# One decoder layer on one core: V and output gate streamed together, GLA output one head later, other starts and ends of stages

## The chip, the cores and the metric

One NeuronCore of a Trainium2 chip runs one program. The metric is the device time of an execution in microseconds (us); lower is better. The kernel before has a median of 1220.12 us over 3 runs (1219.98 to 1223.33).

## What is computed

One layer of a hybrid decoder on x of 512 tokens by 1024 channels, all in float32 (batch 1, depth 1):

```python
h = rms_norm(x, norm_g[0]); proj = h @ w_in            # 1024 x 10816, cut into columns
y_a = rglru_mixer(...)   # conv of width 4, gates by blocks of 128, linear recurrence, GeLU gate
y_b = nsa_mixer(...)     # compressed, selected and window attention, 16 heads of 64
y_c = gla_mixer(...)     # 4 heads, key width 128, value width 256, chunks of 32, silu output gate
merged = sum(gates[i] * (y @ w_branch[i]))             # sigmoid merge gates, three branches
x = x + rms_norm(merged @ w_out, norm_g[1])
h = rms_norm(x, norm_g[2]); gt, up = split(h @ w_ffn_in)
x = x + rms_norm((silu(gt) * up) @ w_ffn_out, norm_g[3])  # d_ff = 2816
```

## The kernel before

All tokens stay on the chip; the weights are streamed. A **piece** of weights is 512 KB: 128 partitions of 1024 float32. SyncE issues its load into a `wraw` buffer (L82), ScalarE (ACT) copies it to a rounded fp32r half `whi` (L91), and VectorE (DVE) subtracts to the rest `wlo` (L92). There are 3 buffers of each, so piece n takes the buffers of piece n - 3. A product with full precision is three fp32r products (`mm3`, L121): high x high, high x low, low x high. Products whose operands were not split (transposes, small attention products) are plain fp32, which TensorE (PE) runs as two passes, each with an instruction of its own in the trace.

The stages, in order of time:
- **Front** (L246 to L309, to 17 us). Four loads bring x in blocks of 128 tokens (`xt0` to `xt3`), then two pieces `ck_raw`, and, from `load_w1(0)` (L391 to L394, called at L676), two loads of 1 MB of `cmp_w1` into the tile `M`, all on SyncE's queue in this order. PE multiplies zeros into a spare bank `WARM` = 14 times (L257). Each block is squared and summed on ACT (`square`), scaled on DVE (`root`, L283) and transposed on PE (L293) as it comes; then ACT and DVE make `hh` and `hl`, the high and low halves of h transposed.
- **NSA** (to 321 us). `small_proj` (L361) computes the 16 low-rank GLA columns and the branch gates; it first copies and adds the low-rank rows (`lr`, L370 to L376), then turns the gates around (`srev`, L379), transposes and gates them (L380 to L382). The attention loop follows with a hand-written order.
- **LRU** (to 477 us). The attention's PSUM pools are closed and others opened (L746 to L751). From here to L1208 the order on PE, DVE, ACT and GpSimd is the order of the code. `take()` (L815) hands out the next piece and has the piece two further split; `stream_t` (L825) multiplies two pieces of weights (stationary, 128x128) by `hh`/`hl` (moving, 512 columns), 48 products, and calls a function of its caller after each piece. `lru_params` (L893), which loads `wr`, makes the small `wa` and two tables of parameters, stands ahead of the loop; `lru_root` and `lru_scan(3)` stand behind it (L1034).
- **GLA** (to 644 us), four heads, each: a q/k stream (`stream_t`), `gla_qk` on DVE (L1052), the transposes of the head before (`gla_turn`, L1140), V by `stream_tok` (L844) with the tokens stationary and 256 columns of weights moving (96 products), `gla_scores` (L1078), the output gate by a second `stream_tok` (96 products), `gla_out` (state products `kvps`, states `ST`, outputs, L1104) and `gla_gate` (L1133). A head's psum tiles rotate through the 4 buffers of `pg`.
- **Merge**, **w_out and norms** (to 870 us), **first FFN product** (to 1100 us).
- **Second FFN product** (L1496 to L1624): a scheme with 7 block products instead of 8. The PSUM pools are closed (L1500) and 8 banks `acc` opened (L1539). `weights()` (L1478) hands out element i of a stream of 40 pieces and has element i + 2 split. The last block product, `p7`, ends with pieces that are held for both token halves (`w3`, L1608); behind its last product come the addition, `gain` (square and sum on ACT, times the norm's gain on DVE, in place), `mean`, `root` and `store` of the last two blocks.

Of the kernel before, what the change touches and what calls it, by code (L numbers as in the profile page):

```python
# [10 lines left out]
F32 = mybir.dt.float32  # L11
# [25 lines left out]
WARM = 14  # L37
# [25 lines left out]
def hybrid_block_kernel(ctx, tc, x, rel_table, norm_g, w_in, conv_w, conv_b, lru_w_gates, lru_b_gates,  # L63
# [181 lines left out]
    x1_d = dram.tile([128, TB, D], F32, name="x1_d")  # L245
    with tc.tile_pool(name="pre", bufs=1) as pp:  # L246
# [25 lines left out]
        with tc.manual_schedule(engines={mybir.EngineType.PE, mybir.EngineType.DVE, mybir.EngineType.Activation}):  # L272
# [88 lines left out]
    def small_proj(pp, ws):  # L361
# [4 lines left out]
        for k in range(8):  # L366
            pe.matmul(sps, w2[:, k], hh[:, k], start=k == 0, stop=False)
            pe.matmul(sps, w2[:, k], hl[:, k], start=False, stop=k == 7)

# [7 lines left out]
        gps = pt.tile([128, TB, 64], F32, name="gtps", tag="pt")  # L377
        srev = pp.tile([128, TB, 128], F32, name="srev", tag="psb", bufs=NPSB)
        v_.tensor_copy(srev, sps.rearrange("p (b c) -> p b c", b=TB)[:, :, ::-1])  # L379
        for tb in range(TB):  # L380
            pe.matmul(gps[:, tb], srev[:, tb], ii, start=True, stop=True)
        a_.activation(gates, gps[:, :, 16:64], AF.Sigmoid)  # L382
# [4 lines left out]
    M = mo_pool.tile([128, 8, S], F32, name="M")  # L387
# [358 lines left out]
    psum_ctx.close()  # L746
    psum_ctx = ExitStack()
    pg = psum_ctx.enter_context(tc.tile_pool(name="pg2", bufs=4, space=PSUM))
    gpools = [(pg, "g"), (pg, "g")]
    pa = psum_ctx.enter_context(tc.tile_pool(name="pa2", bufs=2, space=PSUM))  # L750
    pt = psum_ctx.enter_context(tc.tile_pool(name="pt2", bufs=2, space=PSUM))  # L751
# [31 lines left out]


# [5 lines left out]
    for h in range(4):  # L790
        pieces += in_pieces([(GLA_Q + h * 128, 128), (GLA_K + h * 128, 128)])
        pieces += in_pieces([(GLA_V + h * 256, 256)]) + in_pieces([(GLA_OG + h * 256, 256)])
# [51 lines left out]
    def stream_tok(act, *after):  # L844

        ps = [p.tile([128, 2, 256], F32, name="gps", tag=t) for p, t in gpools]
        both = [ps[tb // 2][:, tb % 2] for tb in range(TB)]
        for kh in range(2):
            for _ in steps_tok(both, take(), kh, act):
                pass  # L850
            if kh < len(after) and after[kh]:
                after[kh]()
        return ps
# [38 lines left out]

    def lru_params():  # L893
        sy.dma_start(wr, gla_wa2[0])
# [120 lines left out]
    lru_params()  # L1015
    for cp in range(4):
# [12 lines left out]
        gate_products(cp)  # L1029
        pm = stream_t(Y[:2], chain(lambda: lru_tanh(cp), *([z_products] if cp == 2 else [])),  # L1030
# [3 lines left out]
    lru_root()  # L1034
    lru_scan(3)
# [16 lines left out]
    def gla_qk(psq, psk, eb, KT, KE):  # L1052
# [3 lines left out]
        QS = gp_.tile([128, 4, 4, CH], F32, name="qs")  # L1056
# [46 lines left out]

    def gla_out(at, QS, KST, V, sfx, psg):  # L1104

        atf = at.rearrange("p b n c -> p b (n c)")
# [5 lines left out]
        for b in (1, 2):  # L1112
            v_.scalar_tensor_tensor(ST[:, b], ST[:, b - 1], sfx[:, b, 0:1], kv[b // 2][:, b % 2], op0=OP.mult,
                                    op1=OP.add)
        O = gp_.tile([128, TB, 256], F32, name="go")
        sg = gp_.tile([128, TB, 256], F32, name="gsg")
        ss = gp_.tile([128, TB], F32, name="gss")
        jk = gp_.tile([128, 256], F32, name="gjk")
        for b2 in range(2):
            a_.activation(sg[:, 2 * b2:2 * b2 + 2], psg[b2], AF.Silu)  # L1120
# [10 lines left out]
        return O, sg, ss  # L1131

    def gla_gate(O, sg, ss):  # L1133
# [28 lines left out]
    held = []  # L1162
    for h in range(4):
        pq = stream_t(hT, gla_consts if h == 0 else None, (lambda: Z.update(x=gla_exp(0))) if h == 0 else None)
        e_ = Z["x"]
        QT, QS, KS, sfx = gla_qk(*pq, *e_)
        if held:
            gla_turn(h - 1, held.pop())
        V = gp_.tile([128, TB, 256], F32, name="gv")
# [3 lines left out]
        pv = stream_tok(hT, sp[0], sp[1])  # L1173
        for b2 in range(2):
            a_.copy(V[:, 2 * b2:2 * b2 + 2], pv[b2])
# [476 lines left out]
```

## Time and profile before

| | us |
|---|---|
| median of 3 runs | 1220.12 |
| runs | 1219.98, 1220.12, 1223.33 |
| profiled execution, its own time | 1221.34 |
| its span, first to last instruction | 1219.6 |
| outside the span | 1.7 |
| PE busy in the span | 1197.8 |
| DVE busy | 656.9 |
| ACT busy | 550.7 |

The profile is of one execution. A PE product in it has a start and a modelled end; products overlap, so the start of one to the start of the next is what a product costs in a stream. An idle time in brackets stands ahead of an instruction, with what ended it. The clock column is the share of TensorE's full clock that was granted: 1.00 is 2.4 GHz, 0.50 is 1.2 GHz.

### The profile page before, as it was taken

The numbers are of one execution on the slowest core, as the hardware profiler recorded it, in microseconds if no ns is written. First come the engines' busy times: TensorE is split into PE (matmuls) and PEld (weight loads), VectorE is DVE, ScalarE is ACT, GpSimd is POOL, SyncE is SP. The second block draws the span as 40 slices with busy tenths as digits, with TensorE's granted clock in tenths as the row PEclk, the third lists the DMA queues.
The fourth block names the chain that finished last, engine by engine and source line by source line (L and its number), as shares of the span: only waits on it lengthen the run. The fifth ranks groups of instructions, "written<-read, shape, count | busy, mean of one in ns | idle before, by whom it ended". The sixth has DMA issues, their size and how long they took to land.

```text
span 1219.6 us, 18072 instructions
## 1 busy us (share of the span) xinstructions
PE 1197.8 (98%) x6834; PEld 1011.7 (83%) x6834; DVE 656.9 (54%) x1308; ACT 550.7 (45%) x1038; POOL 202.9 (17%) x261
## 2 busy tenths in 40 slices
PE   8999999999999999999999999999999999999995
PEld 7897888888788888999998888887988888887884
DVE  5615555555576779465543353446543433446786
ACT  5326556655387676443442233234432323324553
POOL 1224555665101113112221000000000000000000
PEclk8999999999999999999999999999999999999999
DMA  7831422221234547476669334244333333324652
GB/s 248 237 86 29 96 74 66 66 66 53 64 109 130 166 123 228 150 177 145 138 134 207 104 99 160 87 155 138 95 113 87 103 91 100 104 82 159 212 182 91
DMA packets 162102, 151.04 MB, mean 124 GB/s; under 512 B 26706, under 2 KB 139582, under 8 KB 161840
## 3 DMA queue, kind: packets, MB, share of 16 engines
q1 hardware_dynamic: 154912, 125.77, 34.9%
q0 software_dynamic: 6512, 23.07, 8.4%
q8 instruction: 54, 0.88, 0.3%
q10 hardware_dynamic: 592, 1.05, 0.2%
q14 instruction: 32, 0.26, 0.1%
HBM read 145.60 MB, written 27.34 MB: 142 GB/s over the span
## 4 chain that ended last, share of the span: by engine, by line
PE 92%; DVE 4%; ACT 2%; DMA 1%; issue 1%; SPq 0%; DVEq 0%; ACTq 0%
PE gps L836 17%; PE gps L164 14%; PE gps L839 9%; PE gps L122 8%; PE gps L123 7%; PE gps L124 7%; PE gps L167 7%; PE ops L668 4%; PE s L600 3%; PE ptp L646 3%; PE acc L123 3%; PE acc L122 3%; PE acc L124 3%; PE hid L434 1%; PE ops L1125 1%
## 5 line engine op out<-in xcount | busy, mean ns | idle before, releaser
L91 ACT CAST whi<-wraw 128x1024 fp32r<-128x1024 f32 x153 | 159.6, 1049 | 252.2 <-issue 100.7
L92 DVE TENSOR_TENSOR wlo<-wraw,whi 128x1024 fp32r<-128x1024 f32 x131 | 159.9, 1228 | 149.9 <-ACT whi L91 117.9
L164 PE MATMUL gps<-hh,whi 128*128 128x512 f32 x368 | 143.5, 390 | 0.0
L167 PE MATMUL gps<-hl,whi 128*128 128x512 f32 x368 | 143.4, 390 | 0.0
L836 PE MATMUL gps<-hh,whi 128*128 128x512 f32 x320 | 125.4, 392 | 1.6 <-ACT whi L91 1.6
L839 PE MATMUL gps<-hl,whi 128*128 128x512 f32 x320 | 124.6, 389 | 0.0
L122 PE MATMUL gps<-whi,hh 128*128 128x256 f32 x320 | 92.4, 289 | 0.0
L123 PE MATMUL gps<-wlo,hh 128*128 128x256 f32 x320 | 90.6, 283 | 1.4 <-DVE wlo L92 1.4
L164 PE MATMUL gps<-hh,wlo 128*128 128x512 f32 x368 | 90.9, 389 | 0.0
L124 PE MATMUL gps<-whi,hl 128*128 128x256 f32 x320 | 90.5, 283 | 0.0
L164 PEld LDWEIGHTS gps<-hh,whi 128*128 128x128 f32 x368 | 69.1, 188 | 15.0 <-issue 0.9
L167 PEld LDWEIGHTS gps<-hl,whi 128*128 128x128 f32 x368 | 69.1, 188 | 14.5 <-issue 0.2
L164 PEld LDWEIGHTS gps<-hh,wlo 128*128 128x128 f32 x368 | 69.1, 188 | 14.4
L650 DVE COPY psb<-ptp 128x512 f32<-128x512 f32 (+2 forms) x72 | 45.5, 631 | 65.3 <-PE ptp L646 61.6
L611 ACT ACTIVATE p<-p,mx 128x384 f32<-128x384 f32 (+3 forms) x128 | 68.7, 538 | 26.0 <-DVE mx L609 25.9
L836 PE MATMUL gps<-hh,wlo 128*128 128x512 f32 x320 | 79.1, 389 | 0.0
L625 POOL TENSOR_TENSOR p<-p,sc 128x256 f32<-128x256 f32 (+3 forms) x64 | 75.5, 1201 | 1.9
L808 POOL COPY tick<-whi 128x1 f32<-128x1 f32 x44 | 28.0, 636 | 284.2 <-ACT whi L91 284.1
L836 PE MATMUL gps<-yh,whi 128*128 128x512 f32 x192 | 74.8, 390 | 0.0
L839 PE MATMUL gps<-yl,whi 128*128 128x512 f32 x192 | 74.7, 389 | 0.0
L122 PE MATMUL gps<-hh,whi 128*128 128x512 f32 (+1 forms) x176 | 73.8, 420 | 0.1
L836 PEld LDWEIGHTS gps<-hh,whi 128*128 128x128 f32 x320 | 60.1, 188 | 14.5 <-ACT whi L91 2.0
(362 smaller groups left out, 2556.6 us busy)
## 6 DMA issues: line engine op xcount, KB each, us to landing
wraw<-in_w_in_dram SPq DMA_DIRECT2D x60, 512.0 KB, 4.1
wraw<-in_w_ffn_in_dram SPq DMA_DIRECT2D x88, 256.0 KB, 3.2
rows_d<-in_w_ffn_out_dram POOLq DMA_DIRECT2D x22, 512.0 KB, 5.2
cols_d<-in_w_ffn_out_dram POOLq DMA_DIRECT2D x22, 512.0 KB, 6.5
wraw<-in_w_in_dram SPq DMA_DIRECT2D x32, 256.0 KB, 4.1
wraw<-in_w_branch_dram SPq DMA_DIRECT2D x16, 512.0 KB, 3.4
wraw<-in_w_ffn_out_dram SPq DMA_DIRECT2D x18, 256.0 KB, 3.5
bias<-line_d SPq DMA_DIRECT2D x16, 256.0 KB, 4.5
```

The lines of the kernel that those rows point to most:

```text
L91: a_.copy(hi, raw)
L92: lo_eng.tensor_tensor(lo, raw, f(hi), op=OP.subtract)
L122: pe.matmul(ps, lh, rh, start=first, stop=False)
L123: pe.matmul(ps, lh, rl, start=False, stop=False)
L124: pe.matmul(ps, ll, rh, start=False, stop=last)
L164: pe.matmul(ps[n], part_[:, k, c], ah[:, kk], start=kk == 0 and part_ is h, stop=kk == 7 and part_ is l)
L167: pe.matmul(ps[n], h[:, k, c], al[:, kk], start=False, stop=False)
L611: a_.activation(o, o, AF.Exp, scale=-1.0, bias=mx[:, br, gi:gi + 1], accum_out=sm[:, br, gi:gi + 1])
L625: g_.tensor_tensor(o, o, sc[:, br][:, :, None].to_broadcast([128, 2, n]), op=OP.mult)
L668: pe.matmul(ops[h, qb * 128:qb * 128 + 128], v, m, start=first and i == 0, stop=last and i == len(blocks) - 1)
L836: pe.matmul(ps[n], part_[:, k, c], ah[:, kk], start=kk == 0 and part_ is h, stop=kk == 7 and part_ is l)
L839: pe.matmul(ps[n], h[:, k, c], al[:, kk], start=False, stop=False)
```

## The change

- Front: `WARM` becomes 16, and 6 more products of zeros stand between the transposes of block 0 and block 1. `M` is allocated earlier, and two one-column GpSimd copies from `xt3` into `M` stand ahead of the two loads into `M`, which therefore wait until `xt3` has landed.
- `small_proj`: the gates come ahead of the low-rank rows.
- The PSUM pools of the attention are kept to the end; a class `Banks` deals their 8 banks out again (4, 2 and 2, as before).
- `wr` is loaded where it was; `lru_params` runs after the gate products of the first of the four LRU rounds. `lru_root` and `lru_scan(3)` run behind the first piece of head 0's q/k stream, which now stands in the LRU stage.
- V and output gate of a head are one stream: four pieces of 256 rows by 512 columns (256 of V, 256 of the gate), 96 products with 512 columns moving. Tokens 0 to 255 use pieces 0 and 1 first, then tokens 256 to 511; pieces 2 and 3 serve all tokens.
- The states of head h are made inside the q/k stream of head h + 1 (`gla_next`), its outputs behind that stream, its transposes behind the third piece of the next V/gate stream. For head 3 this lies in the merge.
- Second FFN product: no pools closed; a Sqrt at its start; the last element leaves the stream of 40, is loaded and split earlier, into memory that was free; `gain` writes to another tile for half the blocks; `root` and `store` of several blocks come earlier.

```diff
-WARM = 14
+WARM, WARM2 = 16, 6
...
             root(0)
+            for i in range(WARM2):
+                pe.matmul(tps[7][:, 384:512], wz, wz, start=True, stop=True)
...
+            for j8 in range(2):
+                g_.tensor_copy(M[:, 4 * j8, 0:1], xts[TB - 1][:, 0:1])
             root(TB - 1)
...
-    psum_ctx.close()
-    pg = psum_ctx.enter_context(tc.tile_pool(name="pg2", bufs=4, space=PSUM))
+    pg, pa = Banks((pa, "a")), Banks((pg, "g"), (po, "o"))
...
+    def vog_pieces(h):
+        def load(p):
+            aps = [(lambda t, n=n: t.rearrange("p (k c) -> p k c", k=2)[:, :, n * 256:n * 256 + 256],
+                    dap(w_in, p * 256 * INW + c + h * 256, [[INW, 128], [128 * INW, 2], [1, 256]]))
+                   for n, c in enumerate((GLA_V, GLA_OG))]
...
+    def stream_vog(act, *after):
+        ps = [pg.tile([128, S], F32, name="gps", tag="g") for _ in range(TB)]
+        got = []
+        for p, tbs in ((0, (0, 1)), (1, (0, 1)), (0, (2, 3)), (1, (2, 3)), (2, range(TB)), (3, range(TB))):
+            if p == len(got):
+                got.append(take())
+            h, l = got[p]
+            for tb in tbs:
+                t = slice(tb * 128, tb * 128 + 128)
+                for kk in range(2):
+                    k = 2 * p + kk
+                    mm3(ps[tb], ah[:, k, t], al[:, k, t], h[:, kk], l[:, kk], k == 0, k == 7)
+            if TB - 1 in tbs and p < len(after) and after[p]:
+                after[p]()
...
-    lru_params()
...
         gate_products(cp)
+        if cp == 0:
+            lru_params()
...
-    lru_root()
-    lru_scan(3)
+    pq = stream_t(hT, chain(lru_root, lambda: lru_scan(3)))
...
+    def gla_next():
+        G_["st"] = gla_state(G_["kst"], G_["v"], G_["sfx"])
+        if G_["h"] < 3:
+            Z["x"] = gla_exp(G_["h"] + 1)
     for h in range(4):
+        if h:
+            pq = stream_t(hT, gla_next)
         QT, QS, KS, sfx = gla_qk(*pq, *e_)
-        pv = stream_tok(hT, sp[0], sp[1])
+        if h:
+            yt = gla_gate(*gla_out(AT[(h - 1) % 2], G_["qs"], G_["st"], G_["v"]), G_["sg"])
+        if h:
+            sp[2] = chain(*([sp[2]] if sp[2] else []), lambda: gla_turn(h - 1, yt))
+        pv = stream_vog(hT, *sp)
...
+    stream.pop()
...
-        psum_ctx.close()
+        a_.activation(cst[:, 2:3], cst[:, 0:1], AF.Sqrt)
...
+            o = gained[tb, hf] = fp.tile([128, 512], F32, name="fsg", bufs=2) if (hf == 0) == (tb < 2) else c
...
+            if p == 3:
+                raw = raw_tile()
+                sy.dma_start(raw[:, 0:512], cols_d[(2 * NK - 1) * 128:2 * NK * 128])
+            if p == 4:
+                a_.copy(lastw[0][:, :512], raw[:, :512])
+                v_.tensor_tensor(lastw[1][:, :512], raw[:, :512], f(lastw[0][:, :512]), op=OP.subtract)
...
             if p == 2:
                 store(2, 0)
                 store(2, 1)
                 root(3)
+                store(3, 0)
+                store(3, 1)
-        w3 = [weights() for _ in range(3)]
+        w3 = [weights() for _ in range(2)] + [lastw]
...
+            if tt == 0:
+                root(0)
+                store(0, 0)
```

## Rows read from the trace of the kernel before

**Rows 1.** The page: busy us (share of the span) and instructions of PE.

```profile
PE 1197.8 (98%) x6834; PEld 1011.7 (83%) x6834; DVE 656.9 (54%) x1308; ACT 550.7 (45%) x1038; POOL 202.9 (17%) x261
```

**Rows 2.** Waits of PE: us in total, times, longest.

```profile
PE acc L122 <- ACT whi L1433: 1.9, 2, 1.5
PE gps L836 <- ACT whi L91: 1.6, 1, 1.6
PE gps L123 <- DVE wlo L92: 1.4, 1, 1.4
...
PE acc L123 <- DVE wlo L1434: 1.1, 2, 0.8
PE acc L122 <- DVE am L1407: 0.8, 1, 0.8
PE gtps L381 <- DVE srev L379: 0.8, 1, 0.8
```

**Rows 3.** Timeline of PE in the front: start us, us, instruction, count, [idle before].

```profile
1.19 6.00 PE L258 MATMUL gp<-wz 128*128 128x128 f32 x28 [1.19 <-DVE wz L253]
...
10.88 5.38 PE L294 MATMUL tps<-ident,xt 128*128 128x128 f32 x24 [1.88 <-DVE m L280]
16.33 0.77 PE L122 MATMUL gps<-hh,whi 128*128 128x512 f32 x1
```

**Rows 4.** Windows of the front: length, busy by engine, clock, DMA share, GB/s.

```profile
7.10:10.10 3.00, 1.50 (x10) 1.02 (x9) 1.57 (x9) 2.10 (x6) 0.00 (x0) 1.00 1.05 370
10.10:16.90 6.80, 5.95 (x25) 5.48 (x26) 5.80 (x14) 3.76 (x9) 0.51 (x5) 0.50 1.05 351
```

**Rows 5.** Timeline of ACT and DVE in the front.

```profile
8.09 1.06 ACT L278 ACTIVATE jk<-xt 128x1024 f32<-128x1024 f32 x1 [0.85 <-DMA xt<-in_x_dram]
...
12.79 0.81 DVE L292 TENSOR_SCALAR xt<-xt,r,t 128x1024 f32<-128x1024 f32 x1
```

**Rows 6.** Timeline of DVE in the small projection.

```profile
93.97 0.67 DVE L372 TENSOR_TENSOR lr<-lr,sps 16x512 f32<-16x512 f32 x1
```

**Rows 7.** Timeline of ACT at the start of the LRU stage.

```profile
317.65 1.26 ACT L897 CAST wa<-wr 16x512 fp32r<-16x512 f32 x2 [3.13 <-DMA wr<-in_gla_wa_dram]
```

**Rows 8.** Timeline of DVE where the LRU stage ends.

```profile
477.61 1.22 DVE L92 TENSOR_TENSOR wlo<-wraw,whi 128x1024 fp32r<-128x1024 f32 x1
```

**Rows 9.** Timeline of PE: head 1's first q/k product, narrow and wide products.

```profile
508.74 0.58 PE L836 MATMUL gps<-hh,whi 128*128 128x512 f32 x1
...
523.00 0.28 PE L123 MATMUL gps<-wlo,hh 128*128 128x256 f32 x1
523.12 0.28 PE L124 MATMUL gps<-whi,hl 128*128 128x256 f32 x1
...
1197.60 0.39 PE L124 MATMUL acc<-whi,ls 128*128 128x512 f32 x1
1197.82 0.39 PE L122 MATMUL acc<-whi,ls 128*128 128x512 f32 x1
```

**Rows 10.** Timeline of DVE in GLA heads 0 and 1.

```profile
512.76 1.68 DVE L1137 SCALAR_TENSOR_TENSOR gyt<-go,rs_r,gsg 128x256 f32<-128x256 f32 x4
...
519.14 0.69 DVE L1057 SCALAR_TENSOR_TENSOR qt<-gps,eb 128x512 f32<-128x512 f32 x1 [2.44 <-PE gps L836]
...
523.25 0.57 DVE L1075 TENSOR_TENSOR qs<-qt,eb 128x96 f32<-128x96 f32 x3
```

**Rows 11.** Timeline of ACT, then DVE, at the end.

```profile
1194.91 1.28 ACT L1522 ACT_TABLE_LOAD   x1
...
1201.12 1.04 ACT L1433 CAST whi<-am 128x1024 fp32r<-128x1024 f32 x1
...
1210.35 0.69 DVE L1565 TENSOR_TENSOR hl<-acc,hl 128x512 f32<-128x512 f32 x1 [0.56 <-PE acc L124]
...
1212.76 1.40 DVE L1536 SCALAR_TENSOR_TENSOR hl<-hl,rs_r,xr 128x512 f32<-128x512 f32 x2
...
1214.91 1.42 DVE L1536 SCALAR_TENSOR_TENSOR hl<-hl,rs_r,xr 128x512 f32<-128x512 f32 x2
```

More of the change, by code (lines that the diff above doesn't have):

```diff
@@ L245, in hybrid_block_kernel @@
     x1_d = dram.tile([128, TB, D], F32, name="x1_d")
+    M = mo_pool.tile([128, 8, S], F32, name="M")
     with tc.tile_pool(name="pre", bufs=1) as pp:
@@ L842, in stream_t @@
         return ps
[L844 to L852, printed above, removed]
+    def stream_vog(act, *after):
+        ps = [pg.tile([128, S], F32, name="gps", tag="g") for _ in range(TB)]
+        ah, al = act
+        got = []
[10 more added lines that the diff above has]
+                after[p]()
         return ps
@@ L1183, in merge_stream @@
         for c in range(4):
+            first = c == 0 and i == 0
             if c == 0 and i == 2:
@@ L1204, in merge_stream @@
                     v_.tensor_tensor(mT[1][:, k], M[:, k], f(mT[0][:, k]), op=OP.subtract)
+            if first:
+                gla_turn(3, yt)
+                gctx.close()
+                mtp = mtc.enter_context(tc.tile_pool(name="mtp", bufs=1, side="right"))
+                mT.extend(mtp.tile([128, 8, S], F32R, name=n) for n in ("mth", "mtl"))
     merge_stream(0, False)
@@ new lines, in add @@
+        def add(o, x_, y, op=OP.add):
+            v_.tensor_tensor(o, x_, y, op=op)
+        p2, p5 = [[p.tile([128, 512], F32, name="acc", tag=n) for _ in range(2)] for p, n in ((pa, "a"), (pt, "pt"))]
+        p3, p1 = [[pg.tile([128, 512], F32, name="acc", tag="g") for _ in range(2)] for _ in range(2)]
+        p4, p6, p7 = p2, p5, p3
+        for k in range(NK):
+            w = weights()
+            use(p2, LS1[k], 1, w, 0, k)
+            use(p5, LS1[k], 2, w, 1, k)
+            if k == NK - 1:
+                for tt in range(2):
+                    a_.copy(C[2 + tt][:, c0], p2[tt])
+                for tt in range(2):
+                    a_.copy(C[tt][:, c0], p5[tt])
+            w = weights()
+            use(p3, LS1[k], 3, w, 0, k)
+            use(p1, LS1[k], 0, w, 1, k)
+            if k == 0:
+                first_sums(t)
+            elif k == 1:
+                split_ls(LS1[NK - 1], t[:, 0:4], 4)
+            elif k == 2:
+                second_sums(NK - 1, t)
+            if k:
+                second(k - 1)
@@ new lines, in hybrid_block_kernel @@
+        for p in range(NP):
+            w = weights()
+            for k in range(2 * p, min(2 * p + 2, NK)):
+                use(p4, LS2[k], 2, w, k % 2, k)
+            if p == 0:
+                second(NK - 1)
+            if p in (0, 1):
+                add(C[p][:, c1], p3[p], C[p][:, c0])
+                add(C[2 + p][:, c1], p3[p], C[2 + p][:, c0], OP.subtract)
+            if p in (2, 3):
+                add(C[p - 2][:, c0], p1[p - 2], C[p - 2][:, c0], OP.subtract)
+                add(C[p][:, c1], p1[p - 2], C[p][:, c1])
+            if p == 4:
+                for i in range(8):
+                    xres[i // 2, i % 2] = half("xr", i)
+                    sy.dma_start(xres[i // 2, i % 2], x1_d[:, i // 2, i % 2 * 512:i % 2 * 512 + 512])
@@ new lines, in hybrid_block_kernel @@
+        w5 = []
+        for p in range(NP - 3):
+            w = weights()
+            for k in range(2 * p, 2 * p + 2):
+                use(p7, LS2[k], 1, w, k % 2, k)
+            if p in (0, 1):
+                add(C[2 + p][:, c1], p6[p], C[2 + p][:, c1])
+                if p:
+                    root(2)
+                gain(2 + p, 1)
+                mean(2 + p)
+            if p == 2:
+                store(2, 0)
+                store(2, 1)
+                root(3)
+                store(3, 0)
+                store(3, 1)
@@ L1628 @@
+        w3 = [weights() for _ in range(2)] + [lastw]
+        for tt in range(2):
+            for k in range(2 * NP - 6, NK):
+                use(p7, LS2[k], 1, w3[(k - 2 * NP + 6) // 2], k % 2, k, (tt,))
+            add(C[tt][:, c0], p7[tt], C[tt][:, c0])
+            gain(tt, 0)
+            mean(tt)
+            if tt == 0:
+                root(0)
+                store(0, 0)
+        store(0, 1)
+        root(1)
+        store(1, 0)
+        store(1, 1)
+        psum_ctx.close()
 _INS = ['x', 'rel_table', 'norm_g', 'w_in', 'conv_w', 'conv_b', 'lru_w_gates', 'lru_b_gates', 'lru_lambda', 'cmp_pos', 'cmp_w1', 'cmp_w2', 'gla_wa2', 'gla_ba', 'gla_norm', 'w_branch', 'w_out', 'w_ffn_in', 'w_ffn_out']
```

179 lines of the change are left out of this document (57 added, 122 removed).

## The prediction

> **What bounds the kernel now.** I read the page first: PE is busy 98% of the span, every other engine little more than half [rows 1]. So time can come from two places only: products that PE no longer pays for, and the few moments in which PE stands still. The list of PE's waits, read second, gives those moments; six of them lie where the change works [rows 2]. Each costs a little more than its idle time, because in a stream a product that lasts 0.39 us is followed after 0.22 to 0.23 [rows 9]: the last 0.16 of a product, hidden otherwise, stands open in front of a wait. Third come the timelines around each wait, to see what was late and what is late next; fourth, in the front, the clock.
>
> **The parts, one by one.**
>
> *1. Front.* PE has the transposes of block 0 behind it at 9.0, then waits 1.88 us; the clock is at its upper level to 10.1 and at the lower one (0.50, 1.2 GHz) from there to 16.9, after a stretch in which PE was busy 1.5 us of 3.0 [rows 4]. At that level the 24 other transposes take 5.38 us, 0.21 each with DVE's last block done at 13.6 [rows 3, 5], and the first real product takes 0.6 instead of 0.23. Six zero products are 12 passes; 28 passes took 6.00 us, 0.21 each at the lower level [rows 3], so at the upper one about half, 1.3 us: they end at 10.3, inside the wait. If they keep the clock, the last 8 transposes end 0.9 us after DVE's 13.6, at 14.5 instead of 16.26. Not all 1.7 us come through: DVE has a split of 1.2 us (a size like that of [rows 8]) ahead of the first `hl`, so about 0.8 stays, and the faster first product adds up to 0.4. I take 0.9, less than 1.2, since PE idles again between the later transposes and the clock may fall once more. Bounds: if the clock falls all the same, 12 passes at 0.21 run to 11.6 and hold the transposes up by 0.7; so -0.7 to +1.2. The two more warm products (4 passes, 0.9 us at most) fill the 0.4 us before block 0 and end at the upper level; nothing, or 0.4 lost.
>
> *2. The two late loads.* ACT waited 0.85 us for the third block of x [rows 5] while the loads into `M` were already being issued. If those slow the loads of x, up to 0.85 comes back; if not, nothing. I take 0.3, nearer the lower end, since the loads of x stand first in the queue. `M` is used after 41 us and the queue's next loads wait for the front's end at 16.3, so an issue from 9 on is covered by some 25 us; the GpSimd copies (one column each) have nothing urgent behind them. The Trainium skill, "DMA: Bandwidth & Descriptors", section "Queues, rings and completion order", says that each DMA engine consumes the descriptors of one queue in ring order: loads behind x would then not delay it, and this term would be 0 and the sum 0.3 lower; no row here settles it.
>
> *3. Gates first in `small_proj`.* PE waited 0.8 us for `srev` [rows 2], which stood behind an addition of 0.67 on DVE [rows 6], and that behind an ACT copy of the same rows. Without both `srev` is ready about 1.2 us earlier, more than the wait: 0.8 + 0.16, 1.0. Lower bound 0.4, if something else of DVE slips in front. The rows that move back feed only `smallT`, read by the LRU stage 200 us later.
>
> *4. `lru_params` later.* PE's wait of 1.6 us for the first `whi` [rows 2] comes from ACT's queue: the split stood behind `lru_params`, whose copies waited 3.13 us for the small load `wr` [rows 7]. Moved away, the splits run from 314.5 on and PE goes straight on at 321: 1.6 + 0.16, say 1.7. The price appears at the new place: two copies (1.26 [rows 7]) and three changes of ACT's table (1.28 each, as in [rows 11]), some 5.5 us on ACT ahead of the next split. Cover: that piece is needed a whole stream of 48 products later, 48 x 0.227 = 10.9 us. Bounds 0 to 1.75.
>
> *5. Scan inside the q/k stream.* PE waited 1.4 us for the split that started at 477.61 behind the last scan [rows 2, 8]. In the new order the first V/gate piece is split before the scan, the second behind it, ending near 480; PE needs that one after 24 products on half the tokens, 12 x 0.227 = 2.7 us after 477.2, at 479.9. So up to 0.3 may remain: I take 1.5 of 1.6. Bounds 0.5 to 1.6.
>
> *6. Wide products.* A narrow product costs 0.12 us, a wide one 0.227 in the same three-product order, with the stationary tile changed each time [rows 9]. Per head 2 x 96 narrow become 96 wide: 23.04 - 21.76 = 1.28 us, in four heads 5.1. The states move into the middle of the next q/k stream, one more change from fp32 to fp32r products per head; the first product after such a change lasts 0.58 instead of 0.39 [rows 9], so 0.2 x 4 = 0.8 back. I take 4.3; bounds 4.0 to 5.1.
> The Trainium skill, "TensorE: Matmul & The Clock Gate", section "Back-to-back issue gap", gives an isolated gap of N / 2.4 + 2.5 ns, so 109 ns at 256 and 216 at 512 columns: an estimate by it saves 2.5 ns a pair, 1.0 us in all. The rows say 120 and 227; a pair of narrow ones pays 13 ns more than a wide one here, and the measured pair decides.
>
> *7. Order of the GLA heads.* Nothing else of PE's work changes, so this costs nothing where the cover holds. Banks: the next q/k stream needs the banks of tokens 0 to 255, which two silu free; PE has the scores (2.6 us) in between, ACT a table change and two silu of half a bank, about 2.1 us. The splits: see the second rival.
>
> *8. Entry to the second FFN product.* PE waited 0.8 us for the multiplication that frees the last bank of the closing pools [rows 2]; the new first products use banks that have been free since the attention and a piece split earlier: 0.8 + 0.16, 1.0. The Sqrt's table change (1.28) now stands here on ACT ahead of the third piece's split, needed 5.4 us later: nothing.
>
> *9. The end.* Four waits, 1.9 + 1.1 in two pairs [rows 2], lie between the last pieces. The pair of the last single piece (0.4 + 0.3, with 0.16 each about 1.0) goes, as it is split earlier. The larger pair stays in part: its cast ran at 1201.12, behind a table change of 1.28 [rows 11] that goes, and behind `mean(3)`, which now has `root(2)` ahead of it; net 0.8 earlier. PE's last product so ends about 2.0 earlier. But DVE then has four stores (0.7 each, [rows 11]) and `root(3)`, 3.6 us, between the last split and the first addition of p7, and becomes the later one: its last addition comes only 0.8 earlier than 1210.35. Behind that addition the tail was 6.0 us to 1216.33 [rows 11]. It loses one store (0.70) and the in-place multiplication (0.69, as long as that addition), which now runs beside the square: 4.6. Together 0.8 + 1.4 = 2.2; bounds 1.2 to 3.4 (all of PE's 2.0 through).
>
> **Sum.** 0.9 + 0.3 + 1.0 + 1.7 + 1.5 + 4.3 + 1.0 + 2.2 = 12.9 us. The profiled execution took 1221.34, so 1208.4 in its terms; it stood 1.2 above the median of the runs, so 1207.2. The bounds added up give 5 to 16; not all go wrong together, and I count 8.5 to 17 with the runs' own scatter as this case.
>
> **Rivals** (times in terms of the median).
> - *The clock falls anyway* and the front gives nothing or costs 0.7. For it: the later transposes leave PE idle as before. Against: the stretch before the fall is filled. 1207.2 + 1.2 = 1208.4, to 1209.1. Chance 0.12.
> - *GLA waits, slower.* In heads 1 to 3 the split of the third V/gate piece now stands on DVE behind `gla_qk` (519.14 to 523.82, 4.7 us), two multiplications of 0.69, seven small operations of about 0.19, the four that make `gyt` (1.68) and takes 1.2 itself: 10.3 us [rows 8, 10]. Cover: the output products, 14 passes of about 0.21, and 48 wide ones, 13.8 us. Slack 3.5. If DVE comes later than that (ACT's squares and Sqrt are in the chain), PE waits three times: 4.3 us each eats the gain, from 5.5 each the kernel is over 0.3% slower. With 6 each: 1207.2 + 18 = 1225. Chance 0.04; that they are near 4 and the time unchanged, 0.05.
> - *`lru_params` finds no cover:* ACT is nearly full in the first LRU round, so the 1.7 us come back there: 1208.9. Chance 0.08.
> - *The moved steps don't move:* the order between the hand-ordered parts is a planner's, so waits 4 and 5 could stay as they are: 1210.4. Chance 0.05.
> - *Wide products save next to nothing:* the V/gate stream would run at 0.24 a product, as two narrow ones: 1207.2 + 4.3 = 1211.5. Rows 9 speak against it. Chance 0.03. The formula of the Trainium skill's page "TensorE: Matmul & The Clock Gate", cited in part 6, points this way.
>
> **Numbers.** Forecast 0.63; the rivals make up the rest. 0.3%, about what a measurement of this kernel can tell from no change, is 3.7 us. All but the GLA waits lie below 1216.4: faster 0.91, same 0.05, slower 0.04. The range reaches from 17 us gained to the wide-product case: 1203.2 to 1212.
>
> **What would show it.** Right: none of the waits for `srev`, the first `whi`, `wlo` at 477 and the multiplication at 1100 in PE's list; heads 40.5 us apart instead of 41.8; a clock of 1.00 through the transposes and the first product near 15 instead of 16.33; one pair of waits for splits at the end, and a tail of 4.6 us behind DVE's last addition. Wrong: PE waiting for `wlo` or for a bank inside the heads; ACT late in the first LRU round; a new wait for DMA in front.

## The result, and the profile after

The changed kernel takes 1206.61 us (median of 4, 1206.36 to 1206.76); the kernel before took 1220.61 beside it (4 runs, 1219.98 to 1223.33). The ratio is 0.9884, 95% interval 0.9868 to 0.9900: 14.0 us faster. Run once more on another chip (below) it took 1206.72 against 1221.50. The forecast was 1207.2.

The profiled execution has a span of 1204.6 us instead of 1219.6. The page's row for PE, as [rows 1]:

```profile
PE 1189.8 (99%) x6466; PEld 990.7 (82%) x6466; DVE 657.0 (55%) x1308; ACT 554.7 (46%) x1058; POOL 208.8 (17%) x263
```

PE has 368 instructions less: 768 narrow products became 384 wide ones, and 16 passes of zeros came. PE is busy 8.0 us less, and the span fell by 15.0; the other 7 us are idle time that went. PE's list of waits, as [rows 2]:

```profile
PE gp L259 <- DVE wz L254: 1.2, 1, 1.2
PE gps L122 <- DVE hl L313: 0.8, 1, 0.8
PE acc L123 <- DVE wlo L1483: 0.8, 1, 0.8
PE tps L295 <- DVE xt L293: 0.6, 2, 0.3
PE acc L122 <- ACT whi L1482: 0.5, 1, 0.5
```

Of the six waits in [rows 2], those for the first `whi` (1.6), for `wlo` at 477 (1.4), for the multiplication `am` (0.8) and for `srev` (0.8) are gone; of the two pairs at the end one is left, 0.5 and 0.8.

Where the 15.0 us lie is read from the start of the same product in both traces. A real product here is one of full precision: three instructions, the first of them at L122 in the front. Each line is the gain since the line above it:

| stage, up to | before | after | gained in the stage |
|---|---|---|---|
| fourth real product | 18.77 | 16.68 | 2.09 (front) |
| first product behind the gates' | 96.82 | 93.70 | 1.03 (gates first) |
| first gate product of the LRU | 344.77 | 339.71 | 1.94 (`lru_params`) |
| last gate product of the LRU | 455.17 | 449.96 | 0.15 |
| first product of `w_out` | 809.40 | 797.76 | 6.43 (scan, wide products, GLA order) |
| first product of the second FFN product | 1101.11 | 1088.45 | 1.02 (its entry) |
| DVE's last instruction | 1216.32 | 1201.31 | 2.35 (end) |

The front, PE's timeline, as [rows 3], and the window of [rows 4]:

```profile
1.19 5.87 PE L259 MATMUL gp<-wz 128*128 128x128 f32 x32 [1.19 <-DVE wz L254]
...
8.53 1.50 PE L301 MATMUL tps<-wz 128*128 128x128 f32 x12
9.87 1.04 PE L295 MATMUL tps<-ident,xt 128*128 128x128 f32 x8
...
14.50 0.50 PE L122 MATMUL gps<-hh,whi 128*128 128x512 f32 x1 [0.80 <-DVE hl L313]
```
```profile
7.10:10.10 3.00, 2.77 (x24) 2.55 (x25) 2.35 (x12) 2.66 (x8) 0.30 (x2) 1.00 1.05 381
```

(In these rows a product of zeros is two instructions, a transpose one, eight to a block of x; the section on the kernel before counts the transposes among the products of two passes, which the rows don't bear out.) PE is busy 2.77 of these 3.0 us instead of 1.50, and the clock stays at its upper level (1.00, 2.4 GHz) from there to PE's last product. But the loads came earlier too. ACT's square of the third block of x, as [rows 5]:

```profile
6.97 1.06 ACT L279 ACTIVATE jk<-xt 128x1024 f32<-128x1024 f32 x1
```

It starts 1.12 us earlier than 8.09: its wait of 0.85 is gone, and the first block was there 0.29 earlier. So about half of the front's 2.09 us is the clock and half the arrival of x. Whether the change brought either is the first question for the runs.

The end, as [rows 11]: ACT, DVE, and PE's two waits with its last product.

```profile
1187.21 0.20 ACT L1578 ACTIVATE rs_r<-rs_m 128x1 f32<-128x1 f32 x1 [0.78 <-DVE rs_m L1577]
1187.32 1.03 ACT L1482 CAST whi<-am 128x1024 fp32r<-128x1024 f32 x1
```
```profile
1189.52 0.74 DVE L1592 SCALAR_TENSOR_TENSOR hl<-hl,rs_r,xr 128x512 f32<-128x512 f32 x1
...
1193.01 0.68 DVE L1596 TENSOR_TENSOR hl<-acc,hl 128x512 f32<-128x512 f32 x1
...
1196.61 0.68 DVE L1596 TENSOR_TENSOR hl<-acc,hl 128x512 f32<-128x512 f32 x1
...
1200.56 0.74 DVE L1592 SCALAR_TENSOR_TENSOR hl<-hl,rs_r,xr 128x512 f32<-128x512 f32 x1
```
```profile
1188.40 0.50 PE L122 MATMUL acc<-whi,ls 128*128 128x512 f32 x1 [0.50 <-ACT whi L1482]
1189.66 0.50 PE L123 MATMUL acc<-wlo,ls 128*128 128x512 f32 x1 [0.76 <-DVE wlo L1483]
...
1194.78 0.39 PE L124 MATMUL acc<-hh 128*128 128x512 f32 x1
```

The last cast stands behind `mean(3)`'s Sqrt, as the forecast had it. PE ends at 1195.17, yet DVE's addition of that product starts at 1196.61, 1.4 us behind it: DVE has the four stores, `root(3)` and the first half's work ahead of it. Behind that addition the tail is 4.7 us (to 1201.3) instead of 6.0.

### The profile page after: what moved, and what is told of

It reads as the page before. It is cut to its first block, busy times and chain, and to the rows that moved or that the text cites. A ratio compares the mean times of both kernels' runs of the same rounds, so it can differ in the third digit from the quotient of the medians.

```text
span 1204.6 us, 17368 instructions
## 1 busy us (share of the span) xinstructions
PE 1189.8 (99%) x6466; PEld 990.7 (82%) x6466; DVE 657.0 (55%) x1308; ACT 554.7 (46%) x1058; POOL 208.8 (17%) x263
## 4 chain that ended last, share of the span: by engine, by line
PE 94%; DVE 3%; ACT 1%; issue 1%; DMA 0%; DVEq 0%; ACTq 0%
PE gps L859 19%; PE gps L164 14%; PE gps L862 9%; PE gps L122 8%; PE gps L123 7%; PE gps L124 7%; PE gps L167 7%; PE ops L674 4%; PE s L606 3%; PE ptp L652 3%; PE acc L123 2%; PE acc L122 2%; PE acc L124 2%; PE hid L440 1%; PE ops L1157 1%
## 5 line engine op out<-in xcount | busy, mean ns | idle before, releaser
L167 PEld LDWEIGHTS gps<-hl,whi 128*128 128x128 f32 x368 | 69.1, 188 | 14.5 <-issue 0.2
L831 POOL COPY tick<-whi 128x1 f32<-128x1 f32 x44 | 33.8, 769 | 271.8 <-ACT whi L91 271.8
L164 PEld LDWEIGHTS gps<-hh,wlo 128*128 128x128 f32 x368 | 69.1, 188 | 14.3
L122 PE MATMUL gps<-hh,whi 128*128 128x512 f32 (+1 forms) x176 | 73.4, 418 | 0.8 <-DVE hl L313 0.8
L859 PEld LDWEIGHTS gps<-hh,wlo 128*128 128x128 f32 x320 | 60.1, 188 | 12.5
L862 PEld LDWEIGHTS gps<-hl,whi 128*128 128x128 f32 x320 | 60.1, 188 | 12.3
L122 PE MATMUL gps<-whi,hh 128*128 128x512 f32 (+1 forms) x192 | 69.9, 364 | 0.0
```

The costliest lines, as they stand in the source:

```text
L122: pe.matmul(ps, lh, rh, start=first, stop=False)
L164: pe.matmul(ps[n], part_[:, k, c], ah[:, kk], start=kk == 0 and part_ is h, stop=kk == 7 and part_ is l)
L167: pe.matmul(ps[n], h[:, k, c], al[:, kk], start=False, stop=False)
L859: pe.matmul(ps[n], part_[:, k, c], ah[:, kk], start=kk == 0 and part_ is h, stop=kk == 7 and part_ is l)
L862: pe.matmul(ps[n], h[:, k, c], al[:, kk], start=False, stop=False)
```

## The experiments

Twelve runs. Each is the changed kernel with one part undone, unless it says otherwise; the reference for these is the changed kernel's 1206.61 and 1206.72.

**The late loads alone, on the kernel before;** `M` is allocated ahead of the front instead of behind `small_proj`.

```diff
+    M = mo_pool.tile([128, 8, S], F32, name="M")
...
+            for j8 in range(2):
+                g_.tensor_copy(M[:, 4 * j8, 0:1], xts[TB - 1][:, 0:1])
             root(TB - 1)
```

> The kernel before with the two loads into M held back behind the input's last tile, nothing else. Theory (the loads share the DMA engines with x, so holding them back brings the third block of x forward): ACT's square of the third block starts about 1.1 us earlier than 8.09, near 7.0, with no wait for xt, DVE's last scaling of x 0.9 to 1.1 earlier than 12.79, and the whole about 1.0 us faster, 1219.6; the clock still falls near 10. Rival (a queue is consumed in order, loads behind x cannot delay it): square at 8.1, time within 0.2 of before.

1222.59 (11 executions, 1220.79 to 1224.91) against 1222.47 of the kernel before, measured beside it (21 executions, 1219.80 to 1224.40): ratio 1.0004, 95% interval 0.9994 to 1.0014. The loads into `M` were issued at 9.17 instead of 3.95, and the third block of x was late all the same (ACT's timeline):

```profile
7.69 1.06 ACT L279 ACTIVATE jk<-xt 128x1024 f32<-128x1024 f32 x1 [0.58 <-DMA xt<-in_x_dram]
```

The theory falls: the interval excludes the 1.0 us that it had. What made x late in this execution is not the loads behind it: nothing of `M` was under way. The Trainium skill, "DMA: Bandwidth & Descriptors", section "Queues, rings and completion order", says that an engine consumes the descriptors of a queue in ring order, from which the forecast took that later loads don't delay x; this run agrees, though all it shows is that x comes late without them.

This trace holds something else. PE's timeline behind the gates' products, and the window of that stretch (length, busy time and count of PE, PEld, DVE, ACT, POOL, then the clock):

```profile
94.31 1.10 PE L385 MATMUL gtps<-ii,srev 128*128 128x64 f32 x8 [0.84 <-DVE srev L383]
...
96.07 0.79 PE L122 MATMUL gps<-hh,whi 128*128 128x512 f32 x1
```
```profile
95.60:98.90 3.30, 3.30 (x12) 2.57 (x11) 1.25 (x13) 3.27 (x12) 0.00 (x0) 0.50 0.00 0
```

After a wait of 0.84 us for `srev`, the same as in [rows 2], the clock is at its lower level (0.50, 1.2 GHz) in this execution; in the kernel before's profile the same work (96.58 to 99.88) ran at 1.00, with 18 instructions in place of 12. From the first product behind it to the LRU's first gate product the trace needs 1.28 us more (249.23 instead of 247.95). The forecast had priced that wait at its length and 0.16.

**The zeros alone, on the kernel before.**

```diff
-WARM = 14
+WARM, WARM2 = 16, 6
...
             root(0)
+            for i in range(WARM2):
+                pe.matmul(tps[7][:, 384:512], wz, wz, start=True, stop=True)
             square(1)
```

> The kernel before with 16 and 6 products of zeros instead of 14 and none, nothing else. Theory (the zeros alone hold the clock, and the loads alone bring x forward): granted clock 1.00 from about 6 on through the transposes, last transposes near 14.5 (DVE's last scaling stays at 12.8), first real product near 15.4 instead of 16.33, whole 0.9 us faster, 1219.7. Rival (both are needed: with x late the pause before the last blocks is longer and the clock falls all the same): clock 0.50 from some point between 10 and 14, the transposes no earlier, whole 0 to 0.7 slower.

1222.00 (11 executions, 1219.73 to 1224.12), ratio 0.9998, 0.9988 to 1.0008: no difference in time. The clock held in the front, as the theory has it, but x was on time in this profile (third square at 7.08), which the theory did not expect, and so this trace alone can't say what the zeros do.

**The changed kernel without either.**

```diff
-WARM, WARM2 = 16, 6
+WARM, WARM2 = 14, 0
...
-            for j8 in range(2):
-                g_.tensor_copy(M[:, 4 * j8, 0:1], xts[TB - 1][:, 0:1])
```

> The changed kernel with the front as before: 14 products of zeros, no second set, the two loads issued at once. Theory: the fourth real product back at 18.8 (+2.1 us), every later stage shifted by the same, whole 1208.7, 2.1 us over the changed kernel. Rival (the front's gain is swallowed by later waits): less than 1.2 over it.

1206.87 (1206.72 to 1206.97): 0.15 to 0.26 over the changed kernel. The rival's figure, though not its reason: nothing was swallowed later, there was nothing to lose. The fourth product starts at 16.80 (16.68 with the front's changes), x is on time with the loads into `M` issued at once, and with no zeros between the transposes the clock stays up (ACT's timeline, and the window of the transposes):

```profile
7.15 1.06 ACT L279 ACTIVATE jk<-xt 128x1024 f32<-128x1024 f32 x1
```
```profile
10.10:13.60 3.50, 2.90 (x24) 2.41 (x23) 3.32 (x8) 1.52 (x3) 0.00 (x0) 1.00 1.09 373
```

So the 2.09 us of the front in the table above are mostly the difference between two executions, not between two kernels. The last two runs on the front delay x.

**A late x, with and without the zeros.** The first piece of `w_in` (512 KB) goes ahead of the third block of x; the second run has 14 products of zeros and none between.

```diff
         for tb in range(TB):
+            if tb == 2:
+                ck_raw += [load_raw(...)]
             sy.dma_start(xts[tb], x[0, tb * 128:(tb + 1) * 128, :])
```

> The changed kernel with the first 512 KB piece of w_in issued ahead of the third block of x instead of behind the fourth, so that the third block is late in every execution. Theory (the products of zeros between the transposes are there for a late x: they keep the clock while PE waits): ACT's third square at about 8.3 instead of 7.0, granted clock 1.00 throughout, fourth real product about 1.3 later than in the changed kernel, near 18.0, 1208.0 in all. Rival (they don't reach far enough): clock 0.50 from about 10 on, fourth product at 18.8 or later, 1208.8 and over.

> The same with 14 products of zeros and none between the transposes. Theory: clock 0.50 from about 10 on through the transposes, as in the kernel before's profile, fourth product near 18.8 to 19.5, 0.8 to 1.5 us over the run with the zeros. Rival (the clock falls by the moment of the execution, not by the zeros): the two runs within 0.3 of each other, or with the same scatter.

1208.79 (1208.53 to 1209.24) with the zeros, 1208.73 (1208.64 to 1211.18) without. x came later than intended, the third square at 9.17 and 8.52. The clock does what the theory says; PE's timeline and a window, first with the zeros, then without:

```profile
8.62 1.50 PE L305 MATMUL tps<-wz 128*128 128x128 f32 x12
11.96 1.09 PE L299 MATMUL tps<-ident,xt 128*128 128x128 f32 x8 [1.84 <-DVE m L285]
```
```profile
10.10:13.60 3.50, 1.33 (x11) 1.08 (x11) 3.00 (x12) 2.69 (x8) 0.30 (x2) 1.00 0.94 324
```
```profile
11.31 4.51 PE L299 MATMUL tps<-ident,xt 128*128 128x128 f32 x24 [2.36 <-DVE m L285]
```
```profile
11.70:15.00 3.30, 3.30 (x18) 3.16 (x17) 3.10 (x7) 0.85 (x2) 0.00 (x0) 0.50 1.05 354
```

The medians don't separate the two: they lie 0.06 us apart, where the theory had 0.8 to 1.5 and its rival less than 0.3. By time alone the rival stands. In the two traces x's arrival differs by 0.65 us, the late one being the one with the zeros, and that is more than the clock cost; that the other executions differ likewise is not shown. (The 1211.18 has a mean granted clock of 0.995 on record, the three others 0.996 or 0.997.) What does separate them is the time from the third square to the fourth product, in which x's arrival drops out:

| trace | zeros between | ACT's wait for the third block | clock in the transposes | third square to fourth product |
|---|---|---|---|---|
| before | no | 0.85 | 0.50 | 10.68 |
| late loads alone | no | 0.58 | 0.50 | 10.10 |
| late x, no zeros | no | 1.33 | 0.50 | 10.13 |
| changed, no front | no | none | 1.00 | 9.65 |
| zeros alone | yes | none | 1.00 | 9.65 |
| changed | yes | none | 1.00 | 9.71 |
| narrow products (below) | yes | 0.87 | 1.00 | 9.69 |
| late x | yes | 2.15 | 1.00 | 9.70 |

The clock falls where x is late and no zeros stand between the transposes, and in no other of these traces. The six other traces, of runs further down (all with zeros, waits of 0 to 0.35) show no fall in the front either and give 9.69 to 9.71. Without zeros only one trace has x on time. The zeros are worth 0.4 to 1.0 us in an execution with a late x, and nothing in the one with x on time. Nothing shows that holding back the loads into `M` brings x earlier: with them held, and no piece of `w_in` ahead of x, five of nine traces have no wait and four have 0.16 to 0.87; with them issued at once, two of three have none and one has 0.85.

**The changed kernel again,** on the chip of the three that follow.

> The changed kernel once more, on the chip and in the call of the three that follow. Theory (its executions agree, since none loses the clock between the front and the end): 1206.6, all within 0.5 us of each other, granted clock 1.00 from about 6 to 1199. Rival (the narrow scatter of the first four was luck, and the clock falls in some): executions 1 us and more above the lowest. The version without the front's changes took 1206.87 on another chip: if this one stands within 0.4 of it here, the front's changes are worth no more than that.

1206.72 (1206.56 to 1206.81): as the theory has it. The kernel before, measured beside it, spread over 2.7 us (1220.20 to 1222.89).

**The gates behind the low-rank rows again.**

```diff
         lr = pp.tile([16, S], F32, name="lr", tag="t_o", bufs=2)
         ...
         v_.tensor_tensor(smallT[64:80], lr, f(smallT[0:16]), op=OP.subtract)
+        gps = pt.tile([128, TB, 64], F32, name="gtps", tag="pt")
+        ...
+        a_.activation(gates, gps[:, :, 16:64], AF.Sigmoid)
```

> The changed kernel with the gates' products behind the copies of the low-rank rows again. Theory: PE waits about 0.8 us for the reversed copy again, next product at about 94.7 instead of 93.7, 1.0 us in all where the clock holds, 1207.6; in executions where the clock falls in that wait, as in the late-loads run (0.50 from 95.5 to 98.9), another 1.3 us, up to 1208.9, and a wider scatter. Rival (wait hidden later): within 0.3 of the changed kernel.

The four executions took 1207.76, 1207.87, 1209.28 and 1209.31: two at 1.1 over the changed kernel, two at 2.6. The profiled one is of the first two, with the wait back in PE's list and the clock at 1.00:

```profile
PE gtps L387 <- DVE srev L385: 0.8, 1, 0.8
```

Two groups 1.5 us apart are what the fall behind this wait in the late-loads run would make (1.28 by its stage). The record has the mean granted clock of every execution: 0.997 in the first two, 0.996 in the others, as a fall like that one would make it (by estimate, 3.3 us at half the clock in some 1206 take off 0.0014). No trace shows where it fell in this very kernel, so that it was behind this wait is the likeliest reading and not shown. The step is worth 1.0 and more.

**`lru_params` at its old place,** and **the scan ahead of the q/k stream again.**

```diff
+    lru_params()
     for cp in range(4):
...
-        if cp == 0:
-            lru_params()
```
```diff
-    pq = stream_t(hT, chain(lru_root, lambda: lru_scan(3)))
+    lru_root()
+    lru_scan(3)
+    pq = stream_t(hT)
```

> The changed kernel with lru_params at its old place ahead of the first LRU round. Theory: PE waits 1.6 us for the first whi again, first gate products (rips) 1.9 us later than in the changed kernel, 1.9 in all, 1208.5; part of executions 1 us more if the clock falls in the wait. Rival (the step finds no cover at its new place, so the old one costs no more): within 0.5 of the changed kernel.

> The changed kernel with the last root and scan of the LRU ahead of the first q/k stream again. Theory: PE waits 1.4 us for wlo at about 472, then runs on: 1.5 later from there, 1208.1. Rival (planner or piece order gives the time back in the V/gate stream): within 0.5 of the changed kernel.

1208.65 (1208.45 to 1208.99), 1.93 over the changed kernel; 1208.18 (1208.12 to 1208.24), 1.46 over it. Both theories hold; the waits are back, one line from each kernel's list:

```profile
PE gps L859 <- ACT whi L91: 1.6, 1, 1.6
```
```profile
PE gps L123 <- DVE wlo L92: 1.3, 1, 1.3
```

**Narrow products,** everything else as in the changed kernel.

```diff
-                    mm3(ps[tb], ah[:, k, t], al[:, k, t], h[:, kk], l[:, kk], k == 0, k == 7)
+                    for c in (slice(0, 256), slice(256, 512)):
+                        mm3(ps[tb][:, c], ah[:, k, t], al[:, k, t], h[:, kk, c], l[:, kk, c],
+                            k == 0 and c.start == 0, k == 7 and c.start > 0)
```

> The changed kernel with each 512-column product of the V/gate stream issued as two of 256 columns on the same tiles, in the same order: 192 products a head instead of 96. Theory (a narrow pair pays 0.013 us more than a wide one, as 0.120 against 0.227): 96 x 0.013 = 1.28 us a head, 5.1 us in all, 1211.7; heads 41.9 apart instead of 40.6. Rival (the pair costs only 2.5 ns more, as the Trainium skill's isolated issue gap in TensorE: Matmul & The Clock Gate would have it): 1.0 us in all, 1207.6, heads 40.9 apart.

1212.21 (1211.85 to 1212.46): 5.34 over the run without the front's changes, measured beside it, 5.5 to 5.6 over the changed kernel. Two neighbours in PE's timeline, narrow here and wide in the changed kernel:

```profile
485.29 0.28 PE L122 MATMUL gps<-whi,hh 128*128 128x256 f32 x1
485.41 0.28 PE L123 MATMUL gps<-wlo,hh 128*128 128x256 f32 x1
```
```profile
485.13 0.39 PE L123 MATMUL gps<-wlo,hh 128*128 128x512 f32 x1
485.35 0.39 PE L124 MATMUL gps<-whi,hl 128*128 128x512 f32 x1
```

0.120 us against 0.227, over all of the stage's: 384 pairs cost 4.87 us more from the LRU's last gate product to `w_out` (352.67 instead of 347.80), 0.0127 each. The theory holds. (The profiled execution had x late by 0.87, and its fourth product came 1.0 us later than in the changed kernel; that may be what the medians show beyond 4.87, which is not shown.) The estimate of 2.5 ns a pair, worked out from the gap of an isolated product in the Trainium skill's "TensorE: Matmul & The Clock Gate", section "Back-to-back issue gap", would have given 1.0 us; five times that was measured, so for products that change their stationary tile each time the measured pitch decides.

**The old order of the GLA heads, and the old end,** read by stage.

```diff
         G_.update(h=h, kst=KST, v=V, sfx=sfx, qs=QS, sg=sg)
+        gla_next()
+        yt = gla_gate(*gla_out(AT[h % 2], QS, G_["st"], V), sg)
...
-            pq = stream_t(hT, gla_next)
+            pq = stream_t(hT)
```

and the second FFN product's code as in the kernel before, on banks of its own, with one piece more in the stream.

> The changed kernel with two parts undone that lie far apart and are read by stage. (a) State and output products of a GLA head directly behind its scores, wide V/gate products kept. Theory: PE waits for the transposed keys on DVE (scores end 2.6 behind 493.75, the copy 1.8 later) and for the states (about 1.2): 3 us a head, heads 43.5 apart instead of 40.6, 10 to 12 us from the first scores to w_out's first product. Rival (the order costs nothing either way, as the forecast had it for the new order): heads within 0.3 of 40.6. (b) The second FFN product as before, on banks of its own, one piece more in the stream. Theory: first acc product 1.0 later against its stage, from there to DVE's last store 115.2 as before instead of 112.9, 3.4 in all; up to 0.9 more if the clock falls in its waits. Sum over the changed kernel: 13 to 16, so 1220 to 1223. Rival for (b): DVE's stores, not PE's waits, set the end, and it comes to 2 or less.

1217.62 (1216.93 to 1219.70): 10.9 over the changed kernel, where 13 to 16 had been expected. (a) Heads are 42.44 us apart instead of 40.65 (scores to scores, mean of three), and `w_out` starts 7.2 later, 1.8 a head: between theory and rival. The wait for the transposed keys is there as foreseen, 1.6 us four times; the wait for the states that I had added is not, since the output products of the first blocks stand between. (b) The entry costs 0.98 us, and from the first product to DVE's last store 115.18 instead of 112.86: 3.3 in all, as the theory has it. The waits, from PE's list:

```profile
PE kvps L1140 <- DVE kst L1133: 6.4, 4, 1.6
PE acc L122 <- ACT whi L1481: 1.9, 2, 1.5
...
PE acc L123 <- DVE wlo L1482: 1.1, 2, 0.8
PE acc L122 <- DVE am L1455: 0.8, 1, 0.8
```

**The end on three engines,** an attempt to beat both kernels.

```diff
+            if tb > 1:
+                a_.activation(o, gained[tb, hf], AF.Copy, scale=rss[tb][1][:, 0:1])
+                g_.tensor_tensor(o, o, xres[tb, hf], op=OP.add)
+                sy.dma_start(out[0, tb * 128:(tb + 1) * 128, c], o)
+                return
             v_.scalar_tensor_tensor(o, gained[tb, hf], rss[tb][1][:, 0:1], xres[tb, hf], op0=OP.mult, op1=OP.add)
...
-                if p:
-                    root(2)
                 gain(2 + p, 1)
+                ahead(turns[0] + 3)
                 mean(2 + p)
+                if p:
+                    root(2)
```

> The changed kernel with the last four-store knot loosened: the stores of blocks 2 and 3 become an ACT scaling and a GpSimd addition of the residual, and the last two splits are issued ahead of the mean (and its Sqrt) that their casts waited behind. Theory (DVE, 1.4 us behind PE, sets the end, PE's waits of 0.5 and 0.8 come next): PE's last product 1.3 to 1.6 earlier, DVE's last addition directly behind it, 2.6 us earlier than 1196.61, same tail of 4.7: 1204.1. Rival (DVE is not what binds, or GpSimd slows it): last addition no more than 1.4 earlier, 1205.3 or more.

1206.56 (1206.29 to 1206.60): the changed kernel's time. The rival's second half holds. From the stage's first product PE's last one comes 1.4 us earlier (105.34 instead of 106.72), but DVE's last store only 0.4 (112.48 instead of 112.86). PE gave its part; DVE didn't take it. DVE's timeline while GpSimd adds, GpSimd's row, and the shortest, median and longest of its four additions in ns:

```profile
1190.99 0.69 DVE L1601 TENSOR_TENSOR hl<-acc,hl 128x512 f32<-128x512 f32 x1 [0.52 <-PE acc L124]
1191.78 0.69 DVE L1571 TENSOR_TENSOR fsg<-hl,gb 128x512 f32<-128x512 f32 x1
1192.99 0.65 DVE L1575 TENSOR_TENSOR ss<-ssf 128x1 f32<-128x1 f32 x1 [0.52 <-ACT fjk L1570]
...
1194.36 0.51 DVE L1585 SCALAR_TENSOR_TENSOR rs_t<-rs_r,rs_m 128x1 f32<-128x1 f32 x1
...
1195.10 1.00 DVE L1587 TENSOR_TENSOR rs_r<-rs_r,rs_t 128x1 f32<-128x1 f32 x1
```
```profile
1190.59 5.49 POOL L1594 TENSOR_TENSOR hl<-hl,xr 128x512 f32<-128x512 f32 x4 [538.23 <-ACT hl L1593]
```
```profile
L1594 POOL TENSOR_TENSOR hl<-hl,xr x4: 1257/1283/1769, 1190.6 to 1194.8; 128x512 f32<-128x512 f32 x4
```

One-column operations that take 0.15, 0.22 and 0.16 us elsewhere take 0.65, 0.51 and 1.00 here. They end at 1193.64, 1194.87 and 1196.10, each within 0.04 us of the end of a GpSimd addition (windows of 0.04 us count the second one last in 1193.60 to 1193.64 and the third in 1194.84 to 1194.88; the fourth ends at 1196.08): DVE stood until that addition was through. The first addition of p7 came 2.6 us earlier against its stage; of that, 1.6 went so, and 0.5 in waiting for ACT, which has the four scalings ahead of its square.

## Why the prediction was right, and where it was not

The time is within 0.6 us of the forecast, and every wait that was to go went. Two terms were wrong, and they made up for each other; that the sum came so near is in part luck.

**Parts 1 and 2, the front (0.9 and 0.3 forecast).** Between medians they are worth 0.15 to 0.26 together. The step that failed is the first one: part 1 took the fall of the clock in one profiled execution for a property of the kernel, and part 2 did so with x's wait of 0.85. The traces show that x's arrival varies, and, without zeros, the fall with it. The zeros' mechanism was right, and the price of a fall (0.4 to 1.0) near the 0.9, but it is due only in executions with a late x. Part 2's lower end, 0, is the nearest to what the runs show. The 2.09 us in the table of stages look like a forecast surpassed; two profiles of the same stage would have warned.

**Part 3, gates (1.0).** 1.03 by stage; 1.1 in two executions undone, and 2.6 in two. The term missing is a lower clock behind the wait, seen in one trace, of the late-loads run.

**Parts 4 and 5 (1.7 and 1.5).** 1.93 and 1.46. `lru_params` found its cover: PE's only wait in the LRU stage's gate products is 0.4 us for `xl`, as before.

**Part 6, wide products (4.3).** The pitches gave 5.1; 4.9 by stage and 5.3 between medians came. The step that was off is the 0.8 taken off for four more changes between fp32 and fp32r. The changes are there, but nothing is left for them to cost: scan, wide products and order together gave 6.43 in the stage, of which the runs give 1.5 to the scan and 4.9 to the width. Scores to scores, heads are 40.65 us apart instead of 41.84, and 41.86 with narrow products in the new order, so the new order and its changes cost 0.02 a head, not 0.2. PE's timeline at the state products shows what pays, before and after:

```profile
546.47 1.46 PE L1110 MATMUL kvps<-gv,kst 128*128 128x256 f32 x6
547.76 1.03 PE L1125 MATMUL ops<-gv,at 128*128 128x256 f32 x4
```
```profile
542.61 1.46 PE L1140 MATMUL kvps<-gv,kst 128*128 128x256 f32 x6
543.72 0.58 PE L859 MATMUL gps<-hh,whi 128*128 128x512 f32 x1
544.14 0.40 PE L862 MATMUL gps<-hl,whi 128*128 128x512 f32 x1
```

Six fp32 passes with another pass behind them take 1.29 us; with an fp32r product behind them it starts after 1.11, and takes 0.42 to the next one instead of 0.23. What the first product behind a change takes longer, the pass ahead of it takes less; the forecast had counted only the first.

**Part 7, order of the heads (0).** Right, and the old order would have cost 1.8 us a head with wide products. The third piece's split ended in time in head 1:

```profile
517.11 1.22 DVE L92 TENSOR_TENSOR wlo<-wraw,whi 128x1024 fp32r<-128x1024 f32 x1
```

PE needs it 48 products after 511.52, at 522.4: a slack of 4.1 us, 3.5 in the rival's working. That rival (GLA waits, slower) never came near.

**Part 8 (1.0) and part 9 (2.2).** 1.02, and 2.35; undone 0.98 and 2.3. DVE is indeed the later one at the end, by 1.4 us, and the tail behind its last addition is 4.7 where 4.6 was forecast.

**The sum.** 12.9 was forecast. Undone one by one: 0.2 + 1.1 + 1.9 + 1.5 + 5.3 + 1.0 + 2.3 = 13.3, with gates at the price of a clock that holds; 1.5 us more on half of the executions makes it 14.0 on average, beside a measured gain of 14.0 and, on the other chip, 14.8. The difference between the two is the kernel before's: its executions lie between 1219.80 and 1224.40, those of the changed kernel between 1206.36 and 1206.81. The kernel before's scatter goes with the clock. Over the 37 executions of it that were measured beside the experiments, the mean granted clock was 0.996 or 0.997 in the eight shortest (1219.80 to 1220.93) and 0.991 in the five longest (1223.94 to 1224.40). The traces say where it falls: in the front; in the late-loads run also at `srev` and near the end (0.50 from 1204.8 to 1208.3, where the stage of the second product took 0.7 us more than in the profile before); in the run with the zeros alone only near the end (0.50 from 1201.8 to 1205.1, 0.4 us more). The changed kernel's two traces show no fall before 1198, when PE is done. So "1.2 above the median" in the sum's first line was itself the luck of one execution.

## What to carry to other kernels

A wait of PE near 1 us can cost more than its length, in some executions only: see whether the kernel's runs scatter, and look at the granted clock behind each wait in more than one trace before a price is set on it. Where the first microseconds hang on loads, take one profile's front for one draw, and compare stages from an event that doesn't depend on the load. When two engines end close together, freeing one may move nothing, as it did here: read which one issued the last addition, and look at what the engine that is to help shares with it.

## What was not expected of the hardware

- *GpSimd and DVE.* While GpSimd added 128x512 tiles in SBUF, three of DVE's one-column operations on two SBUF operands took 0.51 to 1.00 us instead of 0.15 to 0.22, and each ended with a GpSimd addition. The other way round, three of those additions took 1.26 to 1.28 us and one 1.77: the second, which began within 0.1 us behind the start of DVE's 128x512 multiplication of two SBUF operands, and that kept its 0.69. DVE's addition of a PSUM and an SBUF operand (0.69) and its one-column operations on one operand (0.15, 0.16) were not held up. The Trainium skill says in "SBUF — State Buffer", section "Who interferes with whom", that a DVE instruction with two SBUF inputs contends with a GpSimd instruction that reads SBUF, since its second input comes through a read interface that the two share. The trace agrees; the expectation of the last run had not drawn on it.
- *The clock in the same program.* The kernel before's front ran at 0.50 in one execution and the same instructions, in the changed kernel without the front's changes, at 1.00; the two differ in when the third block of x landed.
